# Even attention: the keys' low part written once per half, and the low product run over the 64 rows that hold the queries' high part

## The chip, the core and the metric

The kernel runs on one core of a Trainium2 chip. The metric is the device time of one execution in microseconds (us); the number that counts is the median of several runs. A profiled execution is one further run, taken by the hardware profiler, with its own time.

## What is computed

The program is two layers of a transformer block on 512 tokens (x) and 256 context tokens (ctx), width 1024, all in float32. The first ("even") layer mixes with a gated MLP over chunks and with differential attention, then comes a SwiGLU; the second ("odd") layer uses windowed attention, and a SwiGLU again. The change lies in the even layer's differential attention:

```python
def diff_attn(q, k, v, lam):
    s = jnp.einsum('bqhd,bkhd->bhqk', q, k).astype(jnp.float32) * ATTN_SCALE
    p = jax.nn.softmax(s, axis=-1).reshape(b, B_HEADS, 2, tq, tk)
    a = p[:, :, 0] - lam * p[:, :, 1]
    return jnp.einsum('bhqk,bkhe->bqhe', a.astype(v.dtype), v)
```

There are 4 heads, each with two pairs of q and k of 64 channels (the two softmaxes that are subtracted). The 512 x-queries see all 768 keys, the 256 context queries see the 256 context keys alone.

## The kernel before

**Number format.** Products of float32 accuracy are made on TensorE from parts: a value is split into a high part (a cast to float32r, on ScalarE) and a low part (value minus high part, on VectorE or GpSimd). An ordinary product is three matmuls (`mm3`, lines 114 to 116: high by high, high by low, low by high).

**Scores.** They use the contraction in another way. A q or k of 64 channels fills only 64 of the 128 rows over which a matmul sums, so the other 64 rows carry a second part. For head t, the tile `qk[t]` holds both 64-channel queries (rows 0 to 63 and 64 to 127), `qk[4+t]` both keys. `stack_q` (lines 267 to 278) makes `qa`, with the first query's high part in rows 0 to 63 and its low part in rows 64 to 127, and `qb`, with the second query's high part in rows 64 to 127 and its low part in rows 0 to 63. `stack_k` (lines 280 to 291) makes for each of the two keys a tile `kh` with the high part in both halves (two ScalarE casts, lines 286 and 287) and a tile `kl` with the low part in both halves (two VectorE subtractions, line 289). A product of `qa` with `kh` over 128 rows then is (high + low query) by high key, and the product of `qa` with `kl` is (high + low query) by low key. The two are summed in PSUM.

**Blocks.** `softmax_diff` (lines 541 to 564) does that for one block of 128 queries: for c = 0 (`qa`) and c = 1 (`qb`) it takes one of two wide PSUM tiles (`pw`), runs the `kh` products (line 552 over 512 keys, line 553 over the 256 context keys) and then the `kl` products, takes the row maximum (VectorE, 554), and the exponential with its sum (ScalarE, 556). Lines 560 to 563 combine the two softmaxes on VectorE. `attend` (566 to 586) takes two blocks at a time, transposes them on TensorE (574), splits them (130, 131) and multiplies with the values (114 to 116 on `pb`). `head` (621 to 638) runs the three pairs of blocks of a head, 0 to 2; the pair 2 holds the context queries, with 256 keys alone. Behind pair 1 it calls `stack` for the next head. Between them lie the norm of the head before (lines 611, 164 to 184, 619), and, as filler for TensorE, the projections of the gated MLP (`gated`, matmuls on `pf`, lines 114 to 116, copied out by ScalarE at 595), weight splits (88, 91), gelu (642, with a table load before and after) and the transposes and statistics of `turn` (654 to 659).

**Order.** Nothing fixes it by hand here: the Tile scheduler places all instructions of an engine in one order, by priorities and by its own timing model. So an edit of one helper can move neighbours on every engine. A tile pool hands out buffers in rotation (`bufs` for each tag); a writer of a buffer waits until the readers of the tile that had it before are done. The stacked key tiles share the tag `sk` with 6 buffers, and one head takes 4: the third and fourth tile of a head reuse the first two of the head before.

Of the kernel before, what the change touches and what calls it, by code (L numbers as in the profile page):

```python
# [6 lines left out]
F32 = mybir.dt.float32  # L7
F32R = mybir.dt.float32r
# [3 lines left out]
ALU = mybir.AluOpType  # L12
AX = mybir.AxisListType.X

P = 128
D = 1024
KT = D // P
TX = 512
TC = 256
TA = TX + TC  # L20
# [7 lines left out]
class Builder:  # L28
# [251 lines left out]
    def stack_k(self, k, pool, T, tag, bufs):  # L280
        nc = self.nc
        out = []
        for X, Y in ((slice(0, 64), slice(64, 128)), (slice(64, 128), slice(0, 64))):
            kh = pool.tile([P, T], F32R, name=self.uid("kh"), tag=tag, bufs=bufs)
            kl = pool.tile([P, T], F32R, name=self.uid("kl"), tag=tag, bufs=bufs)
            nc.scalar.copy(kh[X], k[X])
            nc.scalar.copy(kh[Y], k[X])
            for Z in (X, Y):
                nc.vector.tensor_tensor(kl[Z], k[X], kh[X].bitcast(F32), ALU.subtract)
            out.append((kh, kl))  # L290
        return out


# [38 lines left out]
    def even(self):  # L332
        tc, nc, a = self.tc, self.nc, self.a
# [13 lines left out]
        for k in range(0, KT, 2):  # L347
            t = self.load(Rh, a["xT"][k * P:(k + 2) * P, :].rearrange("(k p) t -> p k t", p=P), [P, 2, TX], f"hx{k}")
# [72 lines left out]
        qk = {}  # L421
# [37 lines left out]
        for half, heads in enumerate(((0, 1), (2, 3))):  # L459
# [3 lines left out]
            for k in range(KT):  # L463
                t = self.adap.tile([P, 2, 512], F32R, name=self.uid("wq"), tag="wq", bufs=3) if k % 3 == 2 else None
# [8 lines left out]
                if half == 0:  # L473
                    t, sh = hx[k], self.modcol(0, 0, k, 0)
# [35 lines left out]
        for k in range(KT):  # L510
            W = self.unit(a["v0"][k * P:(k + 1) * P, :], 512)
            for tb in range(6):
                c = slice(tb * P, (tb + 1) * P)
# [24 lines left out]
        Ra = tc.alloc_tile_pool(name="att0", bufs=1, side="right", reuse_waits="tile")  # L538
        oraw, raw = [], {}

        def softmax_diff(Q, K, qb, eps):


            koff = 0 if qb < 4 else TX
            qs = slice(qb * P, (qb + 1) * P)
            nm, sums = self.small(2, "sa", 10), self.small(2, "sa", 10)
            es = []
            for c in range(2):
                ps = self.wide()
                for p in range(2):  # L550
                    if qb < 4:
                        nc.tensor.matmul(ps[:, :TX], Q[c][:, qs], K[c][p][:, :TX], start=p == 0, stop=p == 1)
                    nc.tensor.matmul(ps[:, TX:TA], Q[c][:, qs], K[c][p][:, TX:], start=p == 0, stop=p == 1)
                nc.vector.tensor_reduce(nm[:, c:c + 1], ps[:, koff:TA], axis=AX, op=ALU.max, negate=True)
                e = Ra.tile([P, TA], F32, name=self.uid("e"), tag="e", bufs=6)
                self.last_exp = nc.scalar.activation(e[:, koff:], ps[:, koff:TA], AF.Exp, bias=nm[:, c:c + 1],
                                                     accum_out=sums[:, c:c + 1])
                es.append(e[:, koff:])
            r = self.small(1, "sa", 10)
            nc.vector.reciprocal(r, sums[:, 1:2])  # L560
            nc.vector.scalar_tensor_tensor(r, r, self.nlam, sums[:, 0:1], ALU.mult, ALU.mult)
            nc.vector.scalar_tensor_tensor(es[0], es[1], r, es[0], ALU.mult, ALU.add)
            nc.vector.scalar_tensor_tensor(eps[:, qb:qb + 1], sums[:, 0:1], EPS, sums[:, 0:1], ALU.mult, ALU.mult)
            return es[0]

        def attend(t, Q, K, qp, o, eps):
            es = [softmax_diff(Q, K, 2 * qp + i, eps) for i in range(2)]
            kbs = list(range(6)) if qp < 2 else [4, 5]
            po = self.bank()[:, :TC]
            for i in range(0, len(kbs), 2):  # L570
                pt = self.bank()
                for j in range(2):
                    for b in range(2):
                        nc.tensor.transpose(pt[:, j * TC + b * P:j * TC + (b + 1) * P],
                                            es[b][:, (i + j) * P:(i + j + 1) * P], self.ident)
                th = Ra.tile([P, 512], F32R, name=self.uid("ath"), tag="at", bufs=6)
                tl = Ra.tile([P, 512], F32R, name=self.uid("atl"), tag="at", bufs=6)
                self.split(th, tl, pt)
                for j in range(2):
                    kb = kbs[i + j]  # L580
                    c = slice(t * P, (t + 1) * P)
                    m = slice(j * TC, (j + 1) * TC)
                    self.mm3(po, (vhi[kb][:, c], vlo[kb][:, c]), (th[:, m], tl[:, m]),
                             i + j == 0, i + j == len(kbs) - 1)
            s = slice(qp * TC, (qp + 1) * TC)
            nc.scalar.copy(o[:, s], po)
# [10 lines left out]

        def stack(t):
            return (self.stack_q(qk[t], Ra, TA, "sq", 3, eng=nc.gpsimd if t == 3 else nc.vector),
                    self.stack_k(qk[4 + t], Ra, TA, "sk", 6))  # L600

        norms = {}

# [17 lines left out]
        def head(t):  # L621
            Q, K = QK.pop(t)
            o = f3("o", 4)
            eps = self.small(6, "sx", 2)
            for qp in range(3):
                attend(t, Q, K, qp, o, eps)
                if qp == 0:
                    norm(t - 1, 1)
                elif qp == 1:
                    if t < 3:  # L630
                        QK[t + 1] = stack(t + 1)
                    norm(t - 1, 2)
            norms[t] = o, eps
            norm(t, 0)
            if t == 3:
                norm(t, 1)
                norm(t, 2)
            oraw.append(o)
# [38 lines left out]
        with tc.high_priority(offset=tc.cur_priority - here):  # L677
            QK = {0: stack(0)}
# [1131 lines left out]
```

## Time and profile before

| | |
|---|---|
| median of 3 runs | 1576.95 us (1575.58 to 1578.64) |
| profiled execution, its own time | 1580.41 us |
| its span, first to last instruction | 1578.6 us |
| mean granted TensorE clock | 0.990 |
| TensorE busy | 1517.3 us, 96% of the span |
| VectorE busy | 1078.7 us, 68% |
| ScalarE busy | 727.8 us, 46% |
| GpSimd busy | 826.8 us, 52% |
| first and last score product of the even attention start | 169.4 us, 301.6 us |

In the profile PE is TensorE's matmuls, PEld its weight loads, DVE VectorE, ACT ScalarE, POOL GpSimd. A row of the timeline has the start, the duration, the engine, the line, the operation, what it writes and reads, and in brackets the idle time before it with the engine, tile and line that ended it. Matmuls are pipelined: the durations of neighbours overlap, and the distance between two starts is what a matmul costs in a dense row. `128*64` at a matmul is the part of the array that it uses, rows by columns. A float32 matmul appears as two records, a float32r matmul as one.

### The profile page before, as it was taken

The page shows a single profiled execution, that of the slowest core. Times are in us where ns is not written, and L with a number is a line of the kernel's source. Part 1 is how long each engine was busy: PE and PEld are TensorE (multiplying, and loading weights), DVE is VectorE, ACT ScalarE, POOL GpSimd, SP SyncE. Part 2 cuts the span into 40 slices and gives each one's busy share as a digit, 9 for nine tenths or more (in the row PEclk, how much of TensorE's full clock was granted, in tenths as well). Part 3 has the DMA queues.
Part 4 walks back from the last instruction along what each step waited for, and adds up shares of the span by engine and source line. Part 5 has one row for each costly group of instructions (what it writes and reads, how often), then busy time and mean ns, then how long its engine had stood idle before and what let it go on. Part 6 is the DMA issues. An engine that isn't in the chain of part 4 may idle for free.

```text
span 1578.6 us, 24990 instructions
## 1 busy us (share of the span) xinstructions
PE 1517.3 (96%) x9563; PEld 1356.5 (86%) x9563; DVE 1078.7 (68%) x1938; ACT 727.8 (46%) x1490; POOL 826.8 (52%) x558
## 2 busy tenths in 40 slices
PE   6999988999999999999999999899999999999998
PEld 4776877889989999999999988677869889999997
DVE  4620788775697787888886486765667876666665
ACT  2422677553552333333333354555645644444444
POOL 0464211050347767767776544531314299898882
PEclk9999998999999999999999999999999999999999
DMA  8735100043123333345542211200225133333201
GB/s 330 310 129 202 44 8 1 1 134 134 67 74 114 113 102 127 127 146 168 162 158 88 79 47 36 66 28 15 68 87 207 48 105 105 105 99 109 93 21 54
DMA packets 53416, 162.27 MB, mean 103 GB/s; under 512 B 6192, under 2 KB 8624, under 8 KB 45616
## 3 DMA queue, kind: packets, MB, share of 16 engines
q1 hardware_dynamic: 46240, 135.37, 25.6%
q10 hardware_dynamic: 7056, 25.30, 4.9%
q8 instruction: 75, 1.23, 0.3%
q14 instruction: 45, 0.37, 0.1%
HBM read 158.55 MB, written 2.10 MB: 102 GB/s over the span
## 4 chain that ended last, share of the span: by engine, by line
PE 85%; DVE 10%; ACT 3%; issue 1%; DMA 0%; POOL 0%; DVEq 0%; SPq 0%; ACTq 0%; POOLq 0%
PE pw L114 12%; PE pw L115 12%; PE pw L116 11%; PE pb L115 8%; PE pb L116 8%; PE pb L114 8%; PE pf L114 4%; PE pf L115 4%; PE pf L116 4%; PE pb L1633 2%; PE pb L1622 2%; PE pf L369 2%; PE pw L1584 1%; PE pw L1592 1%; DVE t L49 1%
## 5 line engine op out<-in xcount | busy, mean ns | idle before, releaser
L115 PE MATMUL pw<-ax,w 128*128 128x384 f32 (+2 forms) x740 | 236.6, 320 | 4.2 <-DVE ax L49 2.2
L114 PE MATMUL pw<-ax,w 128*128 128x384 f32 (+2 forms) x740 | 235.8, 322 | 3.6 <-DVE q L49 1.9
L116 PE MATMUL pw<-ax,w 128*128 128x384 f32 (+2 forms) x740 | 236.1, 320 | 0.1
L784 DVE SCALAR_TENSOR_TENSOR xT<-pb,mod,xT 128x512 f32<-128x512 f32 (+3 forms) x204 | 143.2, 708 | 127.7 <-PE pb L116 127.3
L91 POOL TENSOR_TENSOR w<-raw,w 128x512 fp32r<-128x512 f32 (+1 forms) x76 | 114.9, 1521 | 218.2 <-ACT w L88 195.6
L49 POOL TENSOR_TENSOR w<-raw,w 128x512 fp32r<-128x512 f32 x122 | 185.9, 1539 | 48.5 <-ACT w L49 48.3
L49 POOL TENSOR_TENSOR w<-t,w 128x512 fp32r<-128x512 f32 x99 | 148.7, 1505 | 55.6 <-ACT w L49 55.6
L114 PE MATMUL pb<-hh,w 128*128 128x512 f32 x480 | 170.9, 356 | 2.3 <-DVE xT L784 2.3
L116 PE MATMUL pb<-hh,w 128*128 128x512 f32 x480 | 171.4, 357 | 0.0
L115 PE MATMUL pb<-hh,w 128*128 128x512 f32 x480 | 171.1, 356 | 0.0
L115 PE MATMUL pw<-T,w 128*128 128x384 f32 (+1 forms) x508 | 158.3, 312 | 2.3 <-DVE T L131 2.3
L114 PE MATMUL pw<-T,w 128*128 128x384 f32 (+1 forms) x508 | 157.8, 312 | 2.0 <-ACT T L130 1.5
L116 PE MATMUL pw<-T,w 128*128 128x384 f32 (+1 forms) x508 | 158.2, 312 | 0.0
L115 PEld LDWEIGHTS pw<-ax,w 128*128 128x128 f32 x740 | 140.7, 190 | 10.6 <-DVE ax L49 2.7
L114 PEld LDWEIGHTS pw<-ax,w 128*128 128x128 f32 x740 | 139.8, 190 | 10.8 <-DVE q L49 2.7
L114 PE MATMUL pf<-ax,w 128*128 128x256 f32 (+2 forms) x428 | 141.5, 331 | 4.2 <-ACT f L595 2.8
L116 PEld LDWEIGHTS pw<-ax,w 128*128 128x128 f32 x740 | 140.4, 190 | 3.5 <-DVE w L953 0.4
L115 PE MATMUL pf<-ax,w 128*128 128x256 f32 (+2 forms) x428 | 140.3, 328 | 0.0
L116 PE MATMUL pf<-ax,w 128*128 128x256 f32 (+2 forms) x428 | 140.1, 327 | 0.0
L49 POOL TENSOR_TENSOR hh<-hs,hh 128x768 fp32r<-128x768 f32 (+1 forms) x42 | 78.3, 1866 | 95.0 <-ACT hh L49 93.5
L49 POOL TENSOR_TENSOR w<-rawo,w 128x512 fp32r<-128x512 f32 x59 | 103.6, 1757 | 29.8 <-ACT w L49 29.8
L239 DVE SCALAR_TENSOR_TENSOR junk<-ar,cb 128x1024 bf16<-128x1024 f32 x64 | 105.7, 1651 | 0.0
(410 smaller groups left out, 3920.5 us busy)
## 6 DMA issues: line engine op xcount, KB each, us to landing
raw<-ffn_in SPq DMA_DIRECT2D x44, 1024.0 KB, 5.4
ar<-ada SPq DMA_DIRECT2D x24, 1024.0 KB, 7.4
ar<-ada ACTq DMA_DIRECT2D x48, 512.0 KB, 3.6
rawo<-ffn_out SPq DMA_DIRECT2D x88, 256.0 KB, 3.0
raw<-odd_out SPq DMA_DIRECT2D x32, 256.0 KB, 2.7
raw<-qk SPq DMA_DIRECT2D x16, 256.0 KB, 7.8
raw<-uv SPq DMA_DIRECT2D x16, 256.0 KB, 2.8
raw<-even_out SPq DMA_DIRECT2D x8, 512.0 KB, 3.9
```

Of the source, the lines that this page charges most:

```text
L49: self.tail[key] = fn(*args, **kw)
L91: eng.tensor_tensor(lo, raw, hi.bitcast(F32), ALU.subtract)
L114: mm(out, s[0], m[0], start=start, stop=False, **kw)
L115: mm(out, s[0], m[1], start=False, stop=False, **kw)
L116: return mm(out, s[1], m[0], start=False, stop=stop, **kw)
L239: return self.nc.vector.scalar_tensor_tensor(junk, t, 1.0, self.cb[who], ALU.mult, ALU.mult, accum_out=self.acc[who][:, col:col + 1])
L369: nc.tensor.matmul(ps[32 * q:32 * q + 32, :w], cst[:, k, :], t[:, w * q:w * q + w], start=k == 0, stop=k == KT - 1, skip_group_check=True)
L784: ins = self.nc.vector.scalar_tensor_tensor(h, ps[:, r], self.modcol(l, j, m, who), h, ALU.mult, ALU.add)
L1584: nc.tensor.matmul(ps[:, st:en], Q, K[g][p][:, b0 * P:b1 * P], start=p == 0, stop=p == 1, skip_group_check=True)
L1592: last = nc.tensor.matmul(ps[:, en:en + TC], Q, K[g][p][:, TX:], start=p == 0 and not edge, stop=p == 1, skip_group_check=True)
L1622: last = nc.tensor.transpose(pt[:, x * P:(x + 1) * P], es[2 * (x % 2) + x // 2][:, kb * P:(kb + 1) * P], self.ident)
L1633: nc.tensor.matmul(po[64 * h:64 * h + 64, :], V[vb][:, 64 * g:64 * g + 64], t[:, h * TC:h * TC + TC], start=kb == 0, stop=kb == nb - 1, sk ...
```

## The change

`stack_k` now makes one tile `low` for both keys of a head, with the first key's low part in rows 0 to 63 and the second's in rows 64 to 127, so one VectorE subtraction a key where there were two. The high tiles `kh` stay as they were. `low` has a tag of its own with 2 buffers, `kh` has 4 buffers, so two heads' tiles fit side by side; the memory taken stays at 6 tiles. What `stack_k` returns now names the rows of each product. In `softmax_diff` the first product runs over all 128 rows as before; the second takes rows 0 to 63 of `qa` (or 64 to 127 of `qb`), which hold the query's high part, and the same rows of `low`. The product of the query's low part with the key's low part is no longer computed.

```diff
     def stack_k(self, k, pool, T, tag, bufs):
         nc = self.nc
         out = []
+        low = pool.tile([P, T], F32R, name=self.uid("kl"), tag="kl", bufs=2)
         for X, Y in ((slice(0, 64), slice(64, 128)), (slice(64, 128), slice(0, 64))):
             kh = pool.tile([P, T], F32R, name=self.uid("kh"), tag=tag, bufs=bufs)
-            kl = pool.tile([P, T], F32R, name=self.uid("kl"), tag=tag, bufs=bufs)
             nc.scalar.copy(kh[X], k[X])
             nc.scalar.copy(kh[Y], k[X])
-            for Z in (X, Y):
-                nc.vector.tensor_tensor(kl[Z], k[X], kh[X].bitcast(F32), ALU.subtract)
-            out.append((kh, kl))
+            nc.vector.tensor_tensor(low[X], k[X], kh[X].bitcast(F32), ALU.subtract)
+            out.append(((slice(0, P), kh), (X, low)))
         return out
...
                 ps = self.wide()
-                for p in range(2):
+                for p, (r, k) in enumerate(K[c]):
                     if qb < 4:
-                        nc.tensor.matmul(ps[:, :TX], Q[c][:, qs], K[c][p][:, :TX], start=p == 0, stop=p == 1)
-                    nc.tensor.matmul(ps[:, TX:TA], Q[c][:, qs], K[c][p][:, TX:], start=p == 0, stop=p == 1)
+                        nc.tensor.matmul(ps[:, :TX], Q[c][r, qs], k[r, :TX], start=p == 0, stop=p == 1)
+                    nc.tensor.matmul(ps[:, TX:TA], Q[c][r, qs], k[r, TX:], start=p == 0, stop=p == 1)
...
-                    self.stack_k(qk[4 + t], Ra, TA, "sk", 6))
+                    self.stack_k(qk[4 + t], Ra, TA, "kh", 4))
```

In the built program 80 of the 160 score matmuls of this attention use 64 rows by 128 columns, in 49 groups of one or two that stand between matmuls of the whole array. Their number and their columns are as before. What the scheduler moves is seen best on ScalarE and VectorE. (The lines of the changed kernel have numbers lower by one behind line 286. `f_140` is the key tile of head 2, `f_141` that of head 3, `f_105` of head 1, and `f_103`, `f_138` and `f_139` are query tiles of heads 1, 2 and 3.)

**ScalarE at the end of head 1**, where the context queries' exponentials run. Before:

```order
L556 ACTIVATE e_1852,sa_1847<-pw_1848,sa_1846 128x256
L286 CAST kh_1834<-f_140_887 64x768
L287 CAST kh_1834<-f_140_887 64x768
L272 ACTIVATE qb_1823<-f_138_883 64x768
L556 ACTIVATE e_1858,sa_1847<-pw_1854,sa_1846 128x256
```

Changed:

```order
L555 ACTIVATE e_1843,sa_1838<-pw_1839,sa_1837 128x256
L555 ACTIVATE e_1849,sa_1838<-pw_1845,sa_1837 128x256
L272 ACTIVATE qb_1817<-f_138_883 64x768
L130 CAST ath_1775<-pb_1770 128x512
L555 ACTIVATE e_1862,sa_1857<-pw_1858,sa_1856 128x256
```

The two casts of head 2's second key are gone from between the two exponentials (they stand a head earlier), and the query's multiplication comes behind the second one. The end of head 2 changes in the same way, with the casts of `f_141`.

**ScalarE behind the gelu, at the start of head 2.** Before:

```order
L271 ACTIVATE qa_2378<-f_139_885 64x768
L286 CAST kh_2384<-f_141_889 64x768
L287 CAST kh_2384<-f_141_889 64x768
L130 CAST ath_1811<-pb_1806 128x512
L556 ACT_TABLE_LOAD
```

Changed:

```order
L271 ACTIVATE qa_2369<-f_139_885 64x768
L286 CAST kh_2376<-f_141_889 64x768
L287 CAST kh_2376<-f_141_889 64x768
L286 CAST kh_2380<-f_141_889 64x768
L287 CAST kh_2380<-f_141_889 64x768
L130 CAST ath_1790<-pb_1785 128x512
```

All four casts of head 3's keys now stand here, ahead of the split and the table load, where two stood.

**VectorE at the end of head 0.** Before:

```order
L289 TENSOR_TENSOR kl_1541<-f_105_578,kh_1540 64x768 x2
L275 TENSOR_TENSOR qb_1529<-f_103_574,qb_1529 64x768
L275 TENSOR_TENSOR qa_1822<-f_138_883,qa_1822 64x768
```

Changed:

```order
L288 TENSOR_TENSOR kl_1822<-f_140_887,kh_1823 64x768
L275 TENSOR_TENSOR qb_1526<-f_103_574,qb_1526 64x768
L288 TENSOR_TENSOR kl_1822<-f_140_887,kh_1827 64x768
L275 TENSOR_TENSOR qa_1816<-f_138_883,qa_1816 64x768
```

Head 1's second key is done before the attention starts, and both keys of head 2 stand here, one subtraction each. On TensorE the filler matmuls move against the score products in many places; SP's and GpSimd's rows stand as before.

## The prediction

> **What bounds the kernel now.** I read the page's busy table first, for what the whole program hangs on.
>
> ```profile
> span 1578.6 us, 24990 instructions
> PE 1517.3 (96%) x9563; PEld 1356.5 (86%) x9563; DVE 1078.7 (68%) x1938; ACT 727.8 (46%) x1490; POOL 826.8 (52%) x558
> ```
>
> TensorE is busy for 96% of the span, so work taken from VectorE is worth something only where TensorE waits for it. That is an average over the program; the change touches 158 us of it. So next comes the table of busy time by stretch, cut at the attention's heads: head 0, head 1, head 2, and head 3 with what follows it.
>
> ```profile
> core 0: us, PE busy (x) PEld busy (x) DVE busy (x) ACT busy (x) POOL busy (x), PEclk, DMA share, GB/s
> 169.45:199.67 30.22, 29.60 (x184) 26.10 (x184) 20.46 (x39) 17.52 (x36) 6.65 (x4) 1.00 0.14 40
> 199.67:234.06 34.39, 28.06 (x185) 24.58 (x185) 28.77 (x55) 24.06 (x52) 6.79 (x4) 1.00 0.03 9
> 234.06:278.08 44.02, 37.23 (x199) 31.88 (x200) 37.24 (x101) 31.23 (x60) 6.48 (x4) 0.85 0.00 1
> 278.08:327.20 49.12, 46.49 (x294) 39.97 (x292) 37.27 (x141) 29.34 (x63) 0.00 (x0) 1.00 0.16 53
> ```
>
> Heads 0 and 3 are TensorE's: 29.60 of 30.22 us and 46.49 of 49.12. In heads 1 and 2 it is idle for 6.3 and 6.8 us, with VectorE at 84 and 85%. In head 2 the granted clock is 0.85 besides, a loss of up to 0.15 x 44 = 6.6 us. The timeline of PE shows where the idle time sits:
>
> ```profile
> 201.03 0.49 PE L552 MATMUL pw<-kh,qa 128*128 128x512 f32 x1 [1.37 <-ACT e L556]
> 204.15 0.39 PE L114 MATMUL pf<-ax,w 128*128 128x256 f32 x1 [1.33 <-ACT f L595]
> 232.06 0.39 PE L553 MATMUL pw<-kh,qb 128*128 128x256 f32 x1 [2.54 <-ACT e L556]
> 244.65 0.79 PE L552 MATMUL pw<-kh,qa 128*128 128x512 f32 x1 [1.92 <-ACT e L556]
> 272.19 0.47 PE L552 MATMUL pw<-kh,qa 128*128 128x512 f32 x1 [1.66 <-ACT e L556]
> 274.64 0.72 PE L552 MATMUL pw<-kh,qb 128*128 128x512 f32 x1 [0.96 <-ACT e L556]
> ```
>
> But for 204.15, a score product waits for an exponential that must empty its PSUM tile, near the places where the next head's tiles are stacked.
>
> **The change part by part.** The sum is made against the profiled execution's own 1580.41 us (span 1578.6 and 1.8 around it). The median of the runs is 1576.95, 3.46 lower; I carry the difference over to the median.
>
> *What goes: eight subtractions.* The view of the tile `kl` gives their price and that of the products.
>
> ```profile
> L289 DVE TENSOR_TENSOR kl<-f,kh x16: 942/954/1773, 158.5 to 270.6; 64x768 fp32r<-64x768 f32 x16
> L552 PE MATMUL pw<-kl,qa x16: 391/395/628, 169.9 to 292.7; 128*128 128x512 f32 x16
> L553 PE MATMUL pw<-kl,qa x24: 277/280/415, 170.1 to 300.4; 128*128 128x256 f32 x24
> ```
>
> Eight of the sixteen at 0.954 us are 7.6 us of VectorE. Most of it lies beside TensorE's work. What counts is the chain that ended last, at the ends of heads 1 and 2:
>
> ```profile
> 228.87 0.84 ACT kh L286
> 229.73 0.95 DVE kl L289
> 230.70 0.97 DVE kl L289
> 231.88 0.95 DVE qb L275
> ...
> 269.62 0.95 DVE kl L289
> 270.59 0.95 DVE kl L289
> ```
>
> By the order of the changed program neither key is stacked at these two places any more; only the query remains. At 228.87 this takes up to 0.84 + 0.95 + 0.97 = 2.8 us out of the chain; the query's own 0.95 and its multiplication come into view instead, so I count **2.3 us**. At 269.62 it takes out 1.9 us, and I count **1.9**. What is late next there is the row maximum and the exponential themselves.
>
> *What moves.* The two casts of each second key go a head earlier, since two full sets of buffers exist. The waits of casts for score products go with it, the first row below, 0.9 us in all. At the start of head 2 two more casts now stand ahead of a split and a table load on ScalarE. The second row is the wait of the attention's first product, the last two are the casts:
>
> ```profile
> ACT kh L286 <- PE pw L553: 0.9, 2, 0.5
> PEld pw L552 <- DVE vlo L131: 0.5, 1, 0.5
> ...
> L286 ACT CAST kh<-f x8: 814/830/838, 157.4 to 268.5; 64x768 fp32r<-64x768 f32 x8
> L287 ACT CAST kh<-f x8: 829/831/833, 158.2 to 269.4; 64x768 fp32r<-64x768 f32 x8
> ```
>
> That is 1.66 us later for the exponential for which the product at 244.65 waits, so **+1.7 us**. At the end of head 0 ScalarE has 6 stacking instructions in a row where 4 stood, and 2 fewer just behind; before the attention two casts come earlier and two subtractions go. I count both at nothing: in the first the later stall (the 1.33 us at 204.15) is given back, in the second head 0's first product waited 0.5 us for VectorE's value parts, on a queue that now has 1.9 us less ahead of them. If that cover fails, each costs up to 1.7. No queue of DMAs is touched, and no wait is added: a buffer of `low` or `kh` is taken again two heads later. The sum so far is 1.7 - 2.3 - 1.9 = **-2.5 us**.
>
> *What the 64 rows cost.* No row of this trace has a product over 64 rows, so its price is bounded. A matmul's cost here goes with its columns. Half the rows might halve it: 32 products at 0.23 and 48 at 0.12 would then give back 6.6 us. The rows below speak against it: a product that uses 32 of 128 columns of the array is no shorter per pass, only several run at once. I exclude this gain for that reason. The other end is a change of the array's shape. The trace has such changes, by columns:
>
> ```profile
> 142.65 0.39 PE L114 MATMUL pb<-w,ax 128*128 128x512 f32 x1
> 142.88 0.39 PE L115 MATMUL pb<-w,ax 128*128 128x512 f32 x1
> 143.10 0.39 PE L116 MATMUL pb<-w,ax 128*128 128x512 f32 x1
> 143.42 1.06 PE L369 MATMUL pf<-ar,cst 128*32 128x512 f32 x8
> 144.42 0.50 PE L114 MATMUL pw<-w,ax 128*128 128x512 f32 x1
> 144.75 0.39 PE L115 MATMUL pw<-w,ax 128*128 128x512 f32 x1
> ...
> 285.83 0.86 PE pb L194 x2
> ...
> 1080.77 0.28 PE L115 MATMUL pf<-ax,w 128*128 128x256 f32 x1
> 1080.89 0.28 PE L116 MATMUL pf<-ax,w 128*128 128x256 f32 x1
> 1081.10 0.44 PE L1633 MATMUL pb<-pt,v 128*64 128x256 f32 x2
> ```
>
> From 142.65 to 143.10 are two dense 512-column steps, 0.45 us, so 0.23 each. The first product of another shape starts not 0.23 but 0.32 later: 0.09 lost. At 1081.10 it is 0.21 where 0.12 is due: 0.09 again. The eight records at 143.42 are two rounds of four at once; a round of 512 float32 columns is 0.43 (two take 0.86 at 285.83), so 0.86 of their 1.00 us is work and 0.14 is lost on the way out. Then the next step is 0.33 instead of 0.23: the weight load behind the change was not hidden, another 0.10. Together **0.33 us** for a group. The changed program has 49 groups of 64-row products between whole-array ones, so 49 x 0.33 = 16.2 us of TensorE. A 64-row group loads 128 columns of weights on entry, not 32, so 0.10 rather than some 0.03 may show there too: 0.40 and 19.6 us at the upper end. The lower end is nothing. I take 0.33, the nearest row.
>
> The Trainium skill, TensorEngine Tiling (Array Packing), Key Properties, says that changing the tiling mode, and not just the tile, drains TensorE, and lists 64 x 128 as a mode of its own; by this rule the drains fall due here, while by the column rows taken for columns alone the sum would end at the -2.5 above. The trace agrees for changes of columns (0.09 us each way); no run here yet shows a change of rows.
>
> *How much of it reaches the end.* In heads 0 and 3, where TensorE is dense, all: half of the groups, 8.1 us. In heads 1 and 2 its idle time can take part of it, but ScalarE and VectorE there work on what the scores deliver, so I let half through: 4.0. This is a choice; nothing and all are its ends (0 and 8.1). The sum is 8.1 + 4.0 - 2.5 = **+9.6 us**: 1590.0 for a profiled execution, 1586.5 for the median.
>
> **The rivals.**
>
> *Row groups change for free.* A half-height product might need no change of the array's paths, and its weights load behind the running product. For it: every change of shape in this trace is one of columns. [...] Then the -2.5 stays, and with stalls of 2.5 and 1.7 us shortened some of the half-clock time of head 2 may go; two of the four pieces of about 1.7 us (6.6 by 4) make -5.9: 1571.1. All of them make -9.1: 1567.8. This ends faster. The sign turns at a price of 2.5 / (24.5 + 12.25) = 0.07 us for a group.
>
> *The change of shape costs its gaps alone.* Were the weight loads hidden on both sides, a group would cost 0.09 + 0.09, in all 8.8 us, of which 6.6 reach the end; less 2.5 and the same 3.4 of clock it is +0.7: 1577.7, no change.
>
> *All of it shows.* At 0.40 a group with nothing hidden, no stall shortened, and two more half-clock pieces because TensorE pauses more often: 19.6 + 3.4 = +23: 1600.0.
>
> *The stacking is not ahead at all* (the change doesn't do what it says): if the two keys' halves of one tile were taken as one, a head's first product would wait for both. Both are done a head early by the order, so this costs nothing and is no case of its own.
>
> **How the numbers follow.** Forecast, a full change of shape partly hidden: 0.49. All of it shows: 0.11. Gaps alone: 0.12. Free: 0.28. About 0.2% (3.2 us) is what a measurement of this kernel can tell from no change. So slower has 0.49 + 0.11 = 0.60, the same 0.12, faster 0.28. The likeliest case alone reaches, with 0 to 8.1 let through in heads 1 and 2, the gain between nothing and -2.5, and 0.33 to 0.40 a group, from +5.6 to +19.6: 1582.6 to 1596.6. The range of 8 in 10 takes in the free case but for its end, and the dear one but for its end: 1569.0 to 1598.0.
>
> **What would show each step right or wrong.** In the profile after, the first 64-row product behind a whole-array one starts about 0.32 us after it instead of 0.23, and the second whole-array step behind a group is 0.33; steps of 0.23 there speak for the free case. `kl` has 8 subtractions at 0.95. The waits of 2.54 us (end of head 1) and 1.66 us (end of head 2) fall under 1 us; that at the start of head 2 grows by 1.7. Over the stretch of the attention PE's busy time must grow by some 16 us, or its idle time must. Wrong would be: products over 64 rows that are shorter than 0.23 for 512 columns, a stretch that gets longer while the steps at the groups stay as they were (then the order, not the array, did it), or a different number of half-clock pieces that outweighs the rest.

## The result, and the profile after

| | before | changed |
|---|---|---|
| median of 4 runs | 1577.11 us | 1594.2 us (1592.93 to 1597.13) |
| profiled execution, its own time | 1580.41 us | 1597.13 us |
| its span | 1578.6 us | 1595.3 us |
| mean granted TensorE clock | 0.990 | 0.987 |

The ratio is 1.0107, with a 95% interval of 1.0093 to 1.0122: the change costs 16.9 us (14.7 to 19.2). The forecast was 9.6 us more, so the direction held and the size came out at 1.8 times the forecast.

The busy table of the changed kernel answers to the first lines shown of before. VectorE has 11.6 us less than the 1078.7 of before, TensorE 20.4 us more than 1517.3:

```profile
PE 1537.7 (96%) x9563; PEld 1359.3 (85%) x9563; DVE 1067.1 (67%) x1930; ACT 727.0 (46%) x1490; POOL 825.0 (52%) x558
```

For a comparison by stages one needs cuts at which both kernels have issued the same matmuls; the heads' own borders will not do, because filler moved across them. From the first score product to a filler product behind the attention these are the following stretches, of before (columns: length, then busy time of PE, PEld, DVE, ACT, POOL, the granted clock, DMA):

```profile
169.45:224.93 55.48, 51.92 (x330) 46.00 (x331) 41.23 (x73) 34.70 (x72) 12.15 (x7) 1.00 0.09 27
224.93:272.19 47.26, 38.04 (x223) 32.52 (x222) 39.35 (x104) 35.46 (x69) 6.74 (x5) 0.89 0.00 1
272.19:311.85 39.66, 38.55 (x239) 33.95 (x240) 32.10 (x104) 22.68 (x49) 1.03 (x1) 0.96 0.00 1
sum 142.40, PE 128.51 PEld 112.47 DVE 112.68 ACT 92.85 POOL 19.91; mean PE 42.84 PEld 37.49 DVE 37.56 ACT 30.95 POOL 6.64
```

and of the changed kernel:

```profile
168.93:229.26 60.33, 59.11 (x330) 46.21 (x330) 37.72 (x69) 35.11 (x73) 11.98 (x9) 1.00 0.09 27
229.26:279.68 50.42, 43.64 (x222) 33.08 (x222) 36.70 (x103) 33.19 (x65) 5.88 (x4) 0.86 0.00 0
279.68:326.71 47.03, 44.48 (x241) 34.93 (x241) 31.52 (x102) 21.85 (x49) 0.48 (x1) 0.93 0.00 1
sum 157.78, PE 147.23 PEld 114.22 DVE 105.93 ACT 90.15 POOL 18.35; mean PE 49.08 PEld 38.07 DVE 35.31 ACT 30.05 POOL 6.12
```

157.78 - 142.40 = 15.4 of the 16.7 us between the two profiled executions arise here. TensorE's busy time grows by 18.7, its idle time (length less busy time) shrinks by 3.3, from 13.9 to 10.6. VectorE gives up 6.8 us, near the 7.6 of the eight subtractions. The clock has a part in it: one minus the clock, times the length, is at most 6.8 us of lost time before (0.11 x 47.26 + 0.04 x 39.66) and 10.4 after (0.14 x 50.42 + 0.07 x 47.03).

Where the busy time grows is seen matmul by matmul. The two products of one query with a dense row around them, before:

```profile
174.05 0.28 PE L553 MATMUL pw<-kh,qa 128*128 128x256 f32 x1
174.05 0.19 PEld L552 LDWEIGHTS pw<-kl,qa 128*128 128x128 f32 x1
174.17 0.39 PE L552 MATMUL pw<-kl,qa 128*128 128x512 f32 x1
174.40 0.28 PE L553 MATMUL pw<-kl,qa 128*128 128x256 f32 x1
174.51 0.39 PE L552 MATMUL pw<-kh,qb 128*128 128x512 f32 x1
174.74 0.28 PE L553 MATMUL pw<-kh,qb 128*128 128x256 f32 x1
```

and the same place in the changed kernel:

```profile
174.30 0.28 PE L552 MATMUL pw<-kh,qa 128*128 128x256 f32 x1
174.51 0.18 PEld L551 LDWEIGHTS pw<-kl,qa 64*128 64x128 f32 x1 [0.25 <-issue]
174.51 0.50 PE L551 MATMUL pw<-kl,qa 64*128 64x512 f32 x1
...
174.85 0.27 PE L552 MATMUL pw<-kl,qa 64*128 64x256 f32 x1
175.05 0.19 PEld L551 LDWEIGHTS pw<-kh,qb 128*128 128x128 f32 x1 [0.25 <-issue]
175.05 0.50 PE L551 MATMUL pw<-kh,qb 128*128 128x512 f32 x1
175.38 0.28 PE L552 MATMUL pw<-kh,qb 128*128 128x256 f32 x1
```

From the last whole-array product of one query to that of the next it is 174.74 - 174.05 = 0.69 us before and 175.38 - 174.30 = 1.08 after: **0.39 us for a group**. It comes in four pieces. The first 64-row product starts 0.21 behind its neighbour instead of 0.12, the next one 0.34 behind the first instead of 0.23, the first whole-array one 0.20 instead of 0.12, the one behind it 0.33 instead of 0.23. Two pieces are a drain (0.09 each way), two a weight load that is not hidden (0.11 each way): before, a product's load starts with the matmul ahead of it (174.05) and 0.12 ahead of its own; here a load of the other shape starts with its own matmul (174.51, 175.05). A product over 64 rows itself is no shorter. The unrounded steps give 0.394 for a group and 49 x 0.394 = 19.3 us for all.

### The profile page after: what moved, and what is told of

Read it like the earlier page. It is cut to its first block, busy times and chain, and to the rows that moved or that the text cites. A ratio compares the mean times of both kernels' runs of the same rounds, so it can differ in the third digit from the quotient of the medians.

```text
span 1595.3 us, 24989 instructions
## 1 busy us (share of the span) xinstructions
PE 1537.7 (96%) x9563; PEld 1359.3 (85%) x9563; DVE 1067.1 (67%) x1930; ACT 727.0 (46%) x1490; POOL 825.0 (52%) x558
## 4 chain that ended last, share of the span: by engine, by line
PE 87%; DVE 8%; ACT 3%; issue 1%; DMA 0%; POOL 0%; DVEq 0%; SPq 0%; ACTq 0%; POOLq 0%
PE pw L114 12%; PE pw L115 12%; PE pw L116 12%; PE pb L114 8%; PE pb L115 8%; PE pb L116 8%; PE pf L114 4%; PE pf L115 4%; PE pf L116 4%; PE pb L1632 2%; PE pb L1621 2%; PE pf L368 2%; PE pw L551 2%; PE pw L1583 1%; PE pw L1591 1%
```

## The experiments

Twelve kernels were run, each beside the kernel before on the same chip. The times are ratios to before with their intervals; the last column is the ratio less one, times 1577.1 us.

| run | what it is | ratio, 95% interval | us |
|---|---|---|---|
| changed kernel | | 1.0107 (1.0093 to 1.0122) | +16.9 |
| e1_whole | changed kernel, no 64-row product | 1.0010 (0.9999 to 1.0020) | +1.6 |
| e2_heads03 | 64-row products in heads 0 and 3 | 1.0057 (1.0045 to 1.0070) | +9.0 |
| e3_heads12 | 64-row products in heads 1 and 2 | 1.0062 (1.0048 to 1.0076) | +9.8 |
| e4_elsewhere | before, 49 products of the SwiGLU over 64 rows | 1.0120 (1.0106 to 1.0134) | +18.9 |
| e5_sixteen | e1_whole, each subtraction twice | 1.0036 (1.0024 to 1.0048) | +5.7 |
| e6_pool | e1_whole, second casts on GpSimd | 0.9949 (0.9937 to 0.9961) | -8.0 |
| e7_dve | e1_whole, second casts on VectorE | 0.9982 (0.9971 to 0.9993) | -2.8 |
| e8_rows | before with 64-row products alone | 1.0084 (1.0071 to 1.0097) | +13.2 |
| e9_before_pool | before, second casts on GpSimd | 1.0056 (1.0043 to 1.0069) | +8.8 |
| e10_after_pool | changed kernel, second casts on GpSimd | 1.0081 (1.0067 to 1.0095) | +12.8 |
| e11_three | e1_whole with 3 buffers of `kh` | 1.0017 (1.0006 to 1.0028) | +2.7 |
| e12_pool3 | e1_whole, head 3's second casts on GpSimd | 0.9986 (0.9978 to 0.9995) | -2.2 |

### The array's price against the order: e1_whole, e2_heads03, e3_heads12

The three kernels have the rows of the changed kernel on PE, VectorE and ScalarE in the same order, one by one. Only the rows over which the second product runs differ.

```diff
-            out.append(((slice(0, P), kh), (X, low)))
+            out.append(((slice(0, P), kh), (slice(0, P), low)))
```

> The changed kernel with one word changed: the second score product runs over all 128 rows of `low` again, so no matmul changes the array's shape; tiles, buffers, casts, subtractions and the order on every engine are those of the changed kernel. (It adds the product of a query's low part with the other key's low part, a term of the size of the one that the change drops.) Theory P: each of the 49 groups costs 0.394 us, as read from the steps of the changed kernel's trace (0.093 ahead of the group, 0.106 in it, 0.089 and 0.106 behind it), and all of it reaches the end: 1594.2 - 19.3 = 1574.9 (1573 to 1578, a half-clock piece of 1.7 us more or less). Theory H, as forecast: the groups of heads 1 and 2 reach the end by half: 1594.2 - 9.5 - 4.9 = 1579.8. Theory O: the new order and the buffers made it slower, not the array: within 2 us of 1594.

For two heads alone `stack_k` gets one more argument, here for heads 0 and 3:

```diff
-            out.append(((slice(0, P), kh), (X, low)))
+            out.append(((slice(0, P), kh), (X if half else slice(0, P), low)))
...
-                    self.stack_k(qk[4 + t], Ra, TA, "kh", 4))
+                    self.stack_k(qk[4 + t], Ra, TA, "kh", 4, t in (0, 3)))
```

> The changed kernel with the 64-row product kept in heads 0 and 3 alone (24 of the 49 groups), the other two heads over 128 rows; order as in the changed kernel. P and H agree here: 9.5 us above the kernel without groups (e1_whole), 1584.4 if that is 1574.9. O: no difference to e1_whole.

> The changed kernel with the 64-row product kept in heads 1 and 2 alone (25 groups), heads 0 and 3 over 128 rows; order as in the changed kernel. P: 25 x 0.394 = 9.9 us above e1_whole, the idle time of these heads hides nothing. H: 4.9 above it. If idle time of TensorE hides all of it: 0 above it. O: no difference.

e1_whole stands 1.6 us above before. So the 64 rows cost 16.9 - 1.6 = **15.3 us** (12.5 to 18.1), and theory O, the order, has fallen. By P 1574.9 (a ratio of 0.9986) lies outside e1_whole's interval; H's 1579.8 (1.0017) lies inside it. But the split of H fails: the groups of heads 0 and 3 cost 9.0 - 1.6 = 7.4 us, those of heads 1 and 2 9.8 - 1.6 = 8.2 (each within 2.6), where H had 9.5 and 4.9. Of the price of 9.5 and 9.9 us that is 0.78 and 0.83, each within 0.27: some four fifths reach the end, and no difference between the heads shows. The stretch from the first score product to the same filler product as above shows it for e1_whole:

```profile
169.55:310.77 141.22, 126.68 (x790) 110.62 (x790) 104.75 (x272) 89.46 (x186) 19.07 (x13) 0.96 0.04 12
```

From here to the changed kernel's sum above, with the same rows in the same order, busy time grows by 20.6 us (147.23 - 126.68; 19.3 is the price), and idle time falls from 14.5 to 10.6: 4.0 us are taken up where TensorE waited anyway. The clock is in this too: one minus it, times the length, is 5.6 us here (0.04 x 141.22) against 10.4, so some 5 of the 16.6 us between the two stretches can be the clock's. The share is therefore a rough one.

### The price by itself: e4_elsewhere and e8_rows

```diff
-    def mm3(self, out, s, m, start, stop):
+    def mm3(self, out, s, m, start, stop, r=slice(0, P)):
...
-        return mm(out, s[1], m[0], start=False, stop=stop, **kw)
+        return mm(out, s[1][r], m[0][r], start=False, stop=stop, **kw)
...
-                run("PE", self.mm3, out, (w[:, 0, c], w[:, 1, c]), op[n][j], j == 0 and n in (1, 2, 5), j == 3)
+                run("PE", self.mm3, out, (w[:, 0, c], w[:, 1, c]), op[n][j], j == 0 and n in (1, 2, 5), j == 3, slice(0, 64 if l == 0 and 4 <= f < 11 and j == 1 else P))
```

> The kernel before, with its attention untouched, but with 49 products of the even SwiGLU (the third matmul of 49 of the `mm3`, 384 columns, between whole-array ones) over 64 rows instead of 128; this leaves out half of a low by high term. It stands where TensorE is never idle and no exponential waits for it, and the order of every engine is that of before. P: the price is the array's, 49 x 0.394 = 19.3 us: 1577.1 + 19.3 = 1596.4. If the price were 0.33, as forecast: +16.2, 1593.3. If the cost is one of the attention's chain (scores, maximum, exponential) and not of the array: within 3 us of 1577.

It costs 18.9 us (16.7 to 21.1), 0.386 a group, where P had 19.3 and 0.33 would have given 16.2, outside the interval. TensorE is idle for only 2.5 of 350 us in this stage (the row of 450 to 800 us, further down), so the price is the array's. (The kernel leaves out half of a low by high term.) A lone product there, with its neighbours of 384 columns:

```profile
562.94 0.35 PE L114 MATMUL pw<-T,w 128*128 128x384 f32 x1
563.12 0.34 PE L115 MATMUL pw<-T,w 128*128 128x384 f32 x1
563.39 0.44 PE L116 MATMUL pw<-T,w 64*128 64x384 f32 x1
563.76 0.44 PE L114 MATMUL pw<-T,w 128*128 128x384 f32 x1
564.04 0.34 PE L115 MATMUL pw<-T,w 128*128 128x384 f32 x1
```

The steps are 0.18 where the shape stays, and 0.27, 0.37 and 0.28 around the group: 0.09 + 0.19 + 0.10 more, once more 0.39 within the rounding.

e8_rows undoes the other half of the change: before's 16 subtractions and 6 buffers, with the second product over 64 rows.

```diff
-            out.append((kh, kl))
+            out.append(((slice(0, P), kh), (X, kl)))
...
-                for p in range(2):
+                for p, (r, k) in enumerate(K[c]):
...
-                    nc.tensor.matmul(ps[:, TX:TA], Q[c][:, qs], K[c][p][:, TX:], start=p == 0, stop=p == 1)
+                    nc.tensor.matmul(ps[:, TX:TA], Q[c][r, qs], k[r, TX:], start=p == 0, stop=p == 1)
```

> The kernel before with one part of the change alone: the second product runs over the 64 rows of the query's high part; the 16 subtractions and the 6 buffers stay. The 49 groups are there, the saving is not. If the array's price and the rest of the change add up (15 to 16 us between e1_whole and the changed kernel, 1.7 between before and e1_whole): 15 to 16 us above before, 1593 to 1594. If the price is met in part by other waits in this other order: less, down to +12. If the two-set buffers had hidden some of it: more, up to +19.

It costs 13.2 us (11.2 to 15.3): a little less than expected, with the same 49 groups. In the order of before more of the price falls into TensorE's waits: over the same matmuls its idle time is 155.05 - 148.10 = 7.0 us, where before had 13.9. The clock gives part of it back, 0.92 where before had 0.95 (the mean of its three stretches, by their lengths):

```profile
169.99:325.04 155.05, 148.10 (x789) 115.70 (x790) 114.08 (x279) 93.01 (x189) 18.83 (x12) 0.92 0.04 10
```

### Where the saving went: e5_sixteen, e6_pool, e7_dve

e1_whole has everything that the forecast counted as a gain, and none of the array's price; it should have been 2.5 us faster than before (a ratio of 0.9984, outside its interval; no change, 1, lies just inside). Its chain of waits from the end of head 1 into head 2 says why it is not:

```profile
229.41 0.59 ACT ath L130
...
231.06 1.28 ACT L641
232.35 1.61 ACT f L641 x3
...
235.40 0.73 ACT qa L271
236.13 0.72 ACT kh L286
...
239.31 0.57 ACT ath L130
```

Nearly all of these ten us are ScalarE's: split, exponentials, table load, four gelus, query, four casts, split. The eight subtractions are nowhere in it. The stall of 2.54 us at the end of head 1 is down to 0.61, and the products behind that last split wait instead, 4.99 us:

```profile
227.89 0.39 PE L552 MATMUL pw<-kh,qa 128*128 128x256 f32 x1 [0.61 <-ACT e L555]
...
239.93 0.58 PE L114 MATMUL pb<-ath,vhi 128*128 128x256 f32 x1 [4.99 <-ACT ath L130]
```

In all, idle time is 14.5 us where before had 13.9. This gave theory S: ScalarE's work is the tight spot there, and VectorE's is not. The first test makes the subtractions twice:

```diff
-            nc.vector.tensor_tensor(low[X], k[X], kh[X].bitcast(F32), ALU.subtract)
+            for Z in (X, X):
+                nc.vector.tensor_tensor(low[Z], k[X], kh[X].bitcast(F32), ALU.subtract)
```

> e1_whole (whole-array products, two full sets of key tiles) with each of the 8 subtractions made twice, to the same rows: 16 again, 7.6 us more of VectorE, nothing else added. Theory S: VectorE's 8 subtractions were not on the path; what holds TensorE around the gelu is ScalarE's row of gelu, query, four casts and split (in e1_whole the idle time of 16.0 us of before is 16.5, only moved), so nothing changes: within 2 us of e1_whole. The forecast's theory (1.9 us at two ends of heads come from subtractions): 2 to 4 us above e1_whole.

It is 4.1 us above e1_whole (5.7 - 1.6, within 2.5). The forecast's theory expected 2 to 4, S less than 2, which the lower end of 1.6 just reaches. The scheduler gave it another order in many places on all engines, so the 4.1 us are the subtractions and that order together; which of them was not separated.

The other two take ScalarE's second cast of each key away:

```diff
-            nc.scalar.copy(kh[Y], k[X])
+            nc.gpsimd.tensor_copy(kh[Y], k[X])
```

> e1_whole with the second cast of each key (the copy of the high part into the other half) on GpSimd instead of ScalarE: 8 of ScalarE's casts, 0.83 us each, gone. Theory S: the stall of 4.99 us in front of the first transposed split of head 2's stretch gets shorter by the two casts of 0.83 that stood ahead of it, 1.7 us, and one more us at an end of another head: 2 to 4 us below e1_whole. Rival: GpSimd is slower at it and the products that read the tile then wait for it: as e1_whole or later.

> e1_whole with the second cast of each key on VectorE instead of ScalarE: VectorE has as many instructions for the keys as in the kernel before, ScalarE 8 casts fewer. Theory S: as e6_pool, 2 to 4 us below e1_whole, since VectorE has the room that the subtractions left. Rival (VectorE bounds heads 1 and 2): no gain over e1_whole.

e6_pool is 9.6 us below e1_whole and **8.0 us below before**, the fastest kernel of the study; e7_dve, with `nc.vector` in the same line, is 4.4 below e1_whole. Both directions are as S has them, and e6_pool's size is beyond it (the scheduler moved a few hundred rows in each of the two as well). Its idle time over the same matmuls is 133.07 - 124.33 = 8.7 us where e1_whole has 14.5:

```profile
170.97:304.04 133.07, 124.33 (x790) 109.16 (x791) 105.57 (x272) 86.58 (x181) 23.20 (x16) 0.97 0.03 11
```

The stall at the split shortens to 3.43 us, by nearly the two casts ahead of it, but the score product behind it now waits 1.79 us for an exponential:

```profile
238.14 0.51 PE L114 MATMUL pb<-ath,vhi 128*128 128x256 f32 x1 [3.43 <-ACT ath L130]
240.44 0.79 PE L551 MATMUL pw<-kh,qa 128*128 128x512 f32 x1 [1.79 <-ACT e L555]
```

With the wait for the gelu ahead of it (0.71 here, 0.94 in e1_whole) the place has 5.9 us of waits in both kernels, so it gave nothing. The idle time went elsewhere. e1_whole waits for ScalarE at these two products too, and for 1.10 us at 202.76 and 0.99 at 267.62, and e6_pool has 0.17 us left of the four (at 266.50):

```profile
270.28 0.47 PE L551 MATMUL pw<-kh,qa 128*128 128x512 f32 x1 [1.36 <-ACT e L555]
...
305.16 0.39 PE L114 MATMUL pb<-ath,vhi 128*128 128x256 f32 x1 [1.88 <-ACT ath L130]
```

That is 5.2 of the 5.8 us of idle time, behind heads 0, 2 and 3. So S named the engine rightly and the place wrongly; how much of it is the casts and how much the new order was not separated.

### One place, one buffer, and the other two kernels: e12_pool3, e11_three, e9_before_pool, e10_after_pool

e12_pool3 moves only the two casts that stand ahead of that split (`copy` is a new argument of `stack_k`, in the place of `nc.scalar.copy`):

```diff
-                    self.stack_k(qk[4 + t], Ra, TA, "kh", 4))
+                    self.stack_k(qk[4 + t], Ra, TA, "kh", 4, nc.gpsimd.tensor_copy if t == 3 else nc.scalar.copy))
```

> e1_whole with the second cast on GpSimd for the keys of head 3 alone, the two that stand at the start of head 2 behind the gelu (in the other heads both casts on ScalarE). If e6_pool's gain of 9 to 10 us over e1_whole comes from the stall at that place (4.99 us in e1_whole, 3.43 in e6_pool): 1.7 us of stall and what half-clock time goes with it, 2 to 5 us below e1_whole. If it comes from the ends of all heads alike: a third of the gain or less, about 1 to 3 us.

3.8 us below e1_whole (within 2.1), in the band of the first theory, but the second's 1 to 3 is not excluded either. The waits speak against the place. The one at the split falls to 3.44 us, the score product behind it waits 2.41, and with 0.71 for the gelu that is 6.6 us where e1_whole has 5.9:

```profile
240.53 0.79 PE L551 MATMUL pw<-kh,qa 128*128 128x512 f32 x1 [2.41 <-ACT e L555]
```

What e12_pool3 lacks is the wait of 1.88 us behind head 3, and its clock over the stretch is 0.98 instead of 0.96. The scheduler moved rows here too, so how two casts save 3.8 us stays open.

e11_three puts the second keys' casts back where before has them, with `"kh", 3` in the place of `"kh", 4`.

> e1_whole (whole-array products, 8 subtractions) with 3 buffers of `kh` instead of 4: the second key of the next head then waits, as in the kernel before, for the end of the head, and its two casts stand there again between the exponentials, not a head earlier; ScalarE's row at the start of head 2 is query, two casts, table load. Theory M (standing a head earlier costs, about 5.7 us as between before and e5_sixteen; the 8 subtractions are worth 4): 4 us below before, 5 to 6 below e1_whole. The forecast's theory (it pays to move the casts away from the ends, 2 to 3 us net): 1 to 3 us above e1_whole. Neither: within 2 us of e1_whole, the casts of ScalarE cost the same wherever they stand.

It is 1.1 us above e1_whole (within 2.4). Theory M has fallen; 1.1 lies in the band of the forecast's theory and in that of the third answer, so the run does not decide between a small gain from the earlier casts and none. The waits show an exchange: 2.03 at the end of head 1 and 3.14 at the start of head 2, where e1_whole has 0.61 and 4.99; and 3.08 at the first product of head 1, where e1_whole has 1.10.

The run also tells something that e5_sixteen did not: it has 8 subtractions at before's places, and is no faster than before (+2.7, 0.9 to 4.4).

The edit of e6_pool was then made in the kernel before and in the changed one.

> The kernel before with one edit: the second cast of each key on GpSimd instead of ScalarE (e6_pool without anything of the change). Theory S (ScalarE's casts are the tight spot, and the 8 subtractions beside them are worth 4 us as between e5_sixteen and e1_whole): faster than before by 4 to 6 us, 1571 to 1573, and 3 to 4 us slower than e6_pool. Rival (once ScalarE is relieved, the subtractions are off the path): as e6_pool, 1569. Rival (the gain of e6_pool came from the two full sets): as before, 1577.

All three expectations missed: it is 8.8 us slower than before. With 6 buffers the second key can be cast only when the head's last products have read the tile, so the casts come at the very end of the head (the cast below waits 1.72 us for such a product), where VectorE works on the chain:

```profile
232.10 0.86 POOL L287 CAST kh<-f 64x768 fp32r<-64x768 f32 x1 [7.21 <-issue]
232.18 0.80 DVE L143 TENSOR_SCALAR sm<-sm 128x6 int32<-128x6 int32 x1
...
233.42 1.92 DVE L289 TENSOR_TENSOR kl<-f,kh 64x768 fp32r<-64x768 f32 x2
234.68 1.35 POOL L287 CAST kh<-f 64x768 fp32r<-64x768 f32 x1 [1.72 <-PE pw L553]
235.37 0.67 DVE L147 SCALAR_TENSOR_TENSOR sm<-sm,sm 128x6 f32<-128x6 f32 x1
...
237.14 0.74 DVE L554 TENSOR_REDUCE sa<-pw 128x1 f32<-128x256 f32 x2
...
238.35 0.77 PE L552 MATMUL pw<-kh,qa 128*128 128x512 f32 x1 [2.83 <-ACT e L556]
```

Two instructions of VectorE on six elements, 0.17 and 0.16 us in before, take 0.80 and 0.67 beside GpSimd's casts, and each ends within 0.03 us of its cast (232.96 and 236.03). The row maximum comes behind them and behind three subtractions (the two at 233.42 and the query's at 236.08), and the product at 238.35 waits 2.83 us. So the relief of ScalarE pays together with the change's stacking (two full sets, half the subtractions), not without it. Which of the two it needs was not separated, and the hold on VectorE is read from the trace alone.

> The changed kernel (64 rows) with the second cast of each key on GpSimd: e6_pool with 48 groups of 64-row products. Price theory with everything let through, since e6_pool has only 10.5 us of idle time in the attention: 48 x 0.394 = 18.9 us above e6_pool, 1588. With the share that reached the end between e1_whole and the changed kernel (15 of 19.3 us): +15, 1584. If the relief of ScalarE lets the idle time take up the array's cost: +10 or less, 1579.

20.8 us above e6_pool (within 2.9): by the medians everything is let through, as the first theory has it. e6_pool's idle time of 8.7 us over the same matmuls is hardly drawn on, it is still 148.72 - 140.56 = 8.2 here:

```profile
170.17:318.89 148.72, 140.56 (x789) 109.84 (x790) 105.71 (x272) 87.35 (x181) 22.69 (x16) 0.98 0.03 10
```

But the stretch is only 148.72 - 133.07 = 15.7 us longer than e6_pool's, at nearly the same clock (0.98 and 0.97), so 0.33 us for each of the 48 groups. The two profiled executions are 18.2 us apart, and the rest of this arises outside the attention, where both have the same work. So the pair does not decide between all of the price and some four fifths of it. Against the changed kernel the casts on GpSimd gain 4.1 us (16.9 - 12.8, within 3.2), where they gain 9.6 against e1_whole.

## Why the prediction was right in direction and short in size

The forecast was slower, and slower it is. The sum, term by term:

| term | forecast | measured |
|---|---|---|
| price of a group | 0.33 us, 16.2 in all | 0.39 us, 19.3 in all |
| of it at the end | 12.1 (0.75) | 15.3 (0.79) |
| saved and moved work | -2.5 | +1.6 |
| sum | +9.6 | +16.9 |

**The price of a change of shape: mechanism right, 0.06 us too small.** The forecast built it from a change of columns, 0.09 + 0.14 + 0.10, and named 0.40 as its upper end because a 64-row group loads 128 columns of weights on entry. That is what happens: the load shows on entry as it does on the way out, 0.11 each. The steps named as tests came as named: 0.09 more ahead of the group, 0.33 behind it. The Trainium skill, TensorEngine Tiling (Array Packing), Key Properties, has the drain, and the trace now shows it for rows: 0.09 us each way. (For columns the forecast says 0.09 each way as well, but its own rows have 0.09 on the way in and 0.14 on the way out.) The unhidden load is the larger half. The rivals "free" and "gaps alone" fall with the same rows. 64-row products shorter than 0.23 are not seen (0.34 to the next, 0.11 of it the load).

**The share that reaches the end: right in sum by luck, wrong in place.** All in heads 0 and 3 and half in heads 1 and 2 was a choice; measured is 0.78 and 0.83, with no difference that the intervals tell. The two errors cancel. The reason given against hiding, that ScalarE and VectorE work on what the scores deliver, holds for all heads alike: a later score delays the maximum, the exponential and the next score. And the forecast's cut at 278.08 lies inside head 3: its first score products are those at 272.19 and 274.64, so the waits of 1.66 and 0.96 us stand ahead of head 3's own products and were counted to head 2.

**The gain: this step failed.** Forecast were -2.3 and -1.9 at two ends of heads and +1.7 at the start of head 2. The subtractions went (8 at 0.952 us), and so did the stalls: in the changed kernel the end of head 1 shows 0.90 where 2.54 stood, and 0.47 stands in the place of the 1.66 at the first product of head 3, next to a new 1.04 at the end of head 2.

```profile
234.14 0.38 PE L552 MATMUL pw<-kh,qa 128*128 128x256 f32 x1 [0.90 <-ACT e L555]
...
246.50 0.38 PE L114 MATMUL pb<-ath,vhi 128*128 128x256 f32 x1 [2.45 <-ACT ath L130]
248.59 0.58 PE L115 MATMUL pb<-atl,vhi 128*128 128x256 f32 x1 [1.71 <-DVE atl L131]
...
278.86 0.39 PE L552 MATMUL pw<-kh,qb 128*128 128x256 f32 x1 [1.04 <-ACT e L555]
280.95 0.70 PE L551 MATMUL pw<-kh,qa 128*128 128x512 f32 x1 [0.47 <-ACT e L555]
...
322.60 0.39 PE L114 MATMUL pb<-ath,vhi 128*128 128x256 f32 x1 [1.70 <-ACT ath L130]
```

Of before, these two and the forecast's 244.65 stand at the start of head 2:

```profile
240.41 1.10 PE L194 MATMUL pb<-q,ones 128*128 128x512 f32 x2 [1.10 <-DVE q L184]
242.34 0.39 PE L114 MATMUL pb<-ath,vhi 128*128 128x256 f32 x1 [0.84 <-ACT ath L130]
```

What was late next was in the main not an exponential of the same head but the next work in ScalarE's queue, the gelus and the casts: the wait at the start of head 2 was 3.9 us in before (1.10, 0.84 and 1.92), is 4.2 here (2.45 and 1.71), and 5.9 in e1_whole (4.99 and 0.94). VectorE has a part as well: it ended the 1.10 and the 1.71, and ahead of the latter the changed kernel's chain of waits has two of the remaining key subtractions (at 245.97 and 246.86). And a wait for which the forecast had no term appears behind head 3: 1.70 us for a split that ScalarE reaches only after its gelus (322.60; 1.88 in e1_whole), where before has none. The forecast saw the casts go to the start of head 2 (+1.7; it is +0.3 in the changed kernel and +2.1 in e1_whole) and credited the ends in full beside it, though both stand on one engine's chain a few us apart. That moving ScalarE's work along its own queue only moves the stall is an argument from these waits; e11_three, with the casts moved back, agrees with it (1.1 us, within 2.4), but does not exclude a small gain. What the eight subtractions alone are worth stays open: no gain in e11_three, 4 us in e5_sixteen, each with an order of its own.

**The clock.** The forecast had no term for it in the likeliest case, and two more half-clock pieces of 1.7 us in the dearest. The stretches show 3.6 us more of lost clock time (10.4 against 6.8), as that part of the dearest rival has it, but for one execution each. The changed kernel's is the longest of its four: 1597.13 and 1595.07 us at a mean clock of 0.987, 1593.33 and 1592.93 at 0.991 and 0.992. At the last clock it still stands 15.8 us above before's median, so the clock is a few us of the 16.9 at most. In e1_whole it is as large as what is looked for: four runs of 1577.4 to 1578.4 us at 0.992 to 0.994, seven of 1579.8 to 1583.1 at 0.989 or 0.990. The changes of shape alone do not bring it: with 49 of them in a dense stage the clock stays at 1.00,

```profile
450.00:800.00 350.00, 347.53 (x1872) 308.67 (x1871) 270.15 (x361) 121.22 (x221) 237.50 (x145) 1.00 0.38 125
```

and e10_after_pool has 48 of them in the attention at 0.98. What sets the pieces stays open.

## What to carry to other kernels

Halving the rows of a matmul saves no time on the array and costs 0.39 us each time that it stands between whole-array products; if the other rows can carry anything harmless, fill them (e1_whole does so with one word). Before a saving on one engine is credited at a stall, follow the chain past the stall: if the next work on the same chain belongs to another engine, the time reappears there, and taking work from that engine (here half of ScalarE's casts, to a GpSimd that is half idle) can be the gain, though here it came at other stalls than the one that suggested it. Such a relief can depend on what stands around it: the same line that gave 9.6 us with two sets of tiles and 8 subtractions cost 8.8 us with one and a half sets and 16.

## What the runs showed of the hardware

A weight load for another shape of the array is not taken ahead: it starts with its own matmul (174.51 in the rows above), 0.11 us that a load of the same shape hides. A change of rows costs as much for one product as for two, and as much for 384 columns as for 512 and 256 (0.39 us). VectorE's shortest instructions seem to be held by GpSimd: 0.80 and 0.67 us instead of 0.17 and 0.16 beside casts of 64 x 768 in e9_before_pool, each ending with its cast; no run was made to test it.
